# Seeding the second of seven block products in PSUM, and one order of products and down words for every block of a feed-forward network

## The chip, the cores and the metric

The kernel runs on one core of one Trainium2 chip. The metric is device time in microseconds, the median of several executions. The profile is of one execution. Its engines are named as the profile names them: PE (TensorE, matmuls), PEld (its weight loads), DVE (VectorE), ACT (ScalarE), POOL (GpSimd) and SP (the queue from which most DMA transfers are issued).

## The reference

Two layers, each of a feed-forward network, a mixer and a second feed-forward network, with a layer norm behind each. There are 256 tokens of width 1024, all in float32. The change is in the four feed-forward networks:

```python
def swiglu(x, w_in, w_out):          # w_in: 1024 x 5632, w_out: 2816 x 1024
    gu = x @ w_in
    g, u = gu[..., :D_FF], gu[..., D_FF:]
    return (jax.nn.silu(g) * u) @ w_out

x = layer_norm(ALPHA * x + 0.5 * swiglu(x, ffn_w_in[l, 0], ffn_w_out[l, 0]), ...)
```

The mixers (an mLSTM in layer 0, windowed attention in layer 1) are left alone.

## The kernel before

**Numbers.** Each float32 operand of a matmul is held as two parts, a rounded high part and a low part, which is the remainder. `mm3` (lines 617 to 620) makes a product of three matmuls: high by high, high by low, low by high. A weight word is a tile of 128 x 1024 elements (512 KB). It arrives by DMA into `w_raw` or `s_raw`, ACT casts it to `w_hi`, and DVE subtracts to get `w_lo`. One word feeds 12 matmuls of 512 columns, whether as a quarter of a wide product or as a row of the down projection (a "down word").

**A feed-forward network** (`ffn`, lines 770 to 1052). It begins with the first 512 columns of gate and up (8 words), goes on with 256 more of both (4 words, the "middle"), and does the other 2048 of each in four blocks of 512 (`seven`, lines 946 to 1006). The down projection has 22 words. They are put between the products one by one (`down`, lines 914 to 926), and six are left for the tail, where the layer norm is.

**A block** computes gate and up for both halves of the tokens by seven products in place of eight. Its words are b11 (gate, upper half), b12 (up, upper), b21 (gate, lower) and b22 (up, lower), two words each. The products use sums of words: b11 gets b12, then b22 added by DVE (`s_raw<-s_raw,s_raw`), and is split anew each time. After that DMA adds b21 to it (a transfer on POOL's queue that accumulates). The sums of x on the other side (`S1` to `S4`) are made once per network. The order before is: product 1 (into bank `qa`), `before()`, which turns the last rows of the block ahead by four PE transposes, product 2 (into `qc`), one down word, the products with `S1` (into `qb`) and `S2` (onto `qa`), one down word, those with `S3` and `S4`, one down word, the last product with b11 as DMA has left it, four transposes (`tr`), one down word. The last block of a network leaves out the last two down words. Two down words stand between the middle and block 0.

The gate of the first half of the tokens is product 1 plus product 2. Product 1 is also needed in `qa`, where the `S2` product is added onto it. Before the change ACT copies `qa` to SBUF (`e1`), DVE adds `qc` to it, and ACT takes the Silu of the sum:

```python
def end1():
    v["g0"] = copied(qa, "e1")
def end2():
    W.when_ready(lambda: nc.vector.tensor_add(v["g0"], v["g0"], qc), qc)
```

**What sets the order.** Each engine runs its own list in order. While a network is recorded, `Paced` (lines 65 to 167) keeps a reckoning of when each engine would be done, and after every matmul `Weights.fill` (lines 376 to 400) decides whether a cast, a subtraction or a sum of words is put into the lists of ACT and DVE, earliest due first. The due times follow from `plan`, the list of splits in the order of their use, which the outer `seven` (lines 492 to 524) writes. `Weights.load` (lines 223 to 251) issues the transfers, also by first use. In a network's first part it takes an `s_raw` word only if its place in the plan is less than 12 (`FIRST`) ahead of the words used.

Of the kernel before, what the change touches and what calls it, by code (L numbers as in the profile page):

```python
# [23 lines left out]
SEVENS = 4  # L24
# [40 lines left out]
class Paced:  # L65
# [94 lines left out]
            self.mark(o, self.act + 125)  # L160

    def on_tensor(self, name, n, out, ins):
        self.pe = max(self.pe, self.when(*ins)) + (109.0 if name == "transpose" else n / 2.4 + 13.3)
        for o in out:
            self.mark(o, self.pe + 200)
        if self.filler is not None:
            self.filler()
# [277 lines left out]
def trunk_kernel(ctx: ExitStack, tc: tile.TileContext, x, ffn_w_in, ffn_w_out, ln_g, ln_b, ml_w_in, ml_gate_b,  # L445
# [46 lines left out]
    def seven(w, c0, c1, n, down):  # L492

        def at(r0, c):
            return [two(w, r0 + 256 * j, c) for j in range(2)]

        b12, b11, b22 = ([word(x, 2, TAGS[r]) for x in at(*p)]
                         for r, p in ((2, (0, c1)), (4 if n % 2 else 1, (0, c0)), (3, (512, c1))))
        b21 = at(512, c0)
        full = n < SEVENS - 1  # L500
        half = 1360.0
        s1 = [split_of(w_, None, None, half) for w_ in b11]
        for j in range(2):
            after[s1[j]] = [(b11[j], b12[j]), (b12[j], at(512, c1)[j])]
        for a in b21:
            piece(a, 2, None, half)
        down(1)
        t1 = [split_of(w_, None, p, half, BY_SUM) for w_, p in zip(b11, s1)]
        for j in range(2):
            after[t1[j]] = [(b11[j], b22[j])]  # L510
        t2 = [split_of(w_, None, p, half, BY_SUM) for w_, p in zip(b11, t1)]
        for j in range(2):
            after[t2[j]] = [(b11[j], b21[j])]
        down(1)
        for w_, p in zip(b12, s1):
            split_of(w_, None, p, half, BY_MOVE)
        for w_ in b22:
            split_of(w_, None, None, half)
        if full:
            down(1)  # L520
        for w_, p in zip(b11, t2):
            split_of(w_, None, p, half, BY_MOVE)
        if full:
            down(1)

    ends = {}
    for j, (kind, l, i, _) in enumerate(stages):
        if kind == "ffn":
            wi, wo = ffn_w_in[l, i], ffn_w_out[l, i]
            nth = iter(range(2 * UNITS))  # L530

            def down(n):
                for _ in range(n):
                    rows(wo, next(nth))

            for c0 in (0, F):
                for a in range(4):
                    wide(wi, a * 256, c0)
            for a in range(4):
                beside(wi, a * 256, 512, F + 512)  # L540
            down(2)
            for g in range(SEVENS):
                c0 = 768 + 512 * g
                seven(wi, c0, F + c0, g, down)
            down(6)
        elif kind == "mlstm":
            for c0 in (1024, 1536):
                for a in range(4):
                    wide(ml_w_in[0], a * 256, c0)
            for c0 in range(0, 1024, 256):  # L550
                for a in range(2):
                    narrow(ml_w_in[0], a * 512, c0)
            for c0 in (2048, 2560):
                for a in range(4):
                    wide(ml_w_in[0], a * 256, c0)
            for c in range(8):
                rows(ml_w_out[0], c, (lambda c=c: gcol[:, c:c + 1]))
        else:
            for c0 in (1024, 0):
                for a in range(4):  # L560
                    wide(at_w_in[0], a * 256, c0)
            for c0 in (512, 768):
                for a in range(2):
                    narrow(at_w_in[0], a * 512, c0)
            for c in range(8):
                rows(at_w_out[0], c)
        ends[j] = len(words)
# [28 lines left out]
    nc.vector.tensor_scalar(ident, ji, 0.0, None, op0=OP.is_equal)  # L596
    mhalf = consts.tile([128, 2], F32, name="mhalf")
    nc.gpsimd.memset(mhalf, -0.5)

    gcol = consts.tile([128, 8], F32, name="gcol")  # L600
    gw = consts.tile([128, 8, 16], F32, name="gw")
# [168 lines left out]
    def ffn(l, i, n, pending, last):  # L770
        with ExitStack() as ph:
# [18 lines left out]
            def tr(hB, t, h):  # L790
                p = wbank((128, 4, 128))
                for k in range(4):
                    nc.tensor.transpose(p[:, k], h[:, k * 128:(k + 1) * 128], ident)
                split_evac(pair(hB, A, A, tok(t)), p, wait=True)

            def chunks(hB, n_):
# [117 lines left out]
            def down(n_):  # L914
                if not y:
                    y.extend([ybank() for _ in range(2)] for _ in range(2))
                W.flush()
                for _ in range(n_):
                    c = done_[0]
                    w, = W.take(1)  # L920
                    for t in range(2):
                        for o in range(2):
                            mm3(y[t][o], pair(hT[c], A, tok(t)), pair(w, A, 0, slice(o * 512, o * 512 + 512)),
                                c == 0, False)
                    W.done()
                    done_[0] += 1
# [3 lines left out]
            def product(bank, x_of, first, then):  # L930

                for j in range(2):
                    w, = W.take(1)
                    for k in range(2):
                        mm3(bank, x_of(2 * j + k), pair(w, A, k), first and j == k == 0, j == k == 1, not first)
                then()
                W.done()

            def copied(bank, name):
                e = temp(name)  # L940
                nc.scalar.copy(e, bank)
                return e
# [3 lines left out]
            def seven(full, before):  # L946

                of = lambda k0, t: (lambda k: pair(xT, A, k0 + k, tok(t)))
                sum_ = lambda name: (lambda k: pair(xs[name], A, k))
                v = {}  # L950
                hB = h_room(4)
                chunks(hB, 4)
                qa, qc = wbank(), wbank()

                def end1():
                    v["g0"] = copied(qa, "e1")

                def end2():
                    W.when_ready(lambda: nc.vector.tensor_add(v["g0"], v["g0"], qc), qc)

                def end5():
                    v["u1"] = copied(qb, "e5")

                def end6():
                    v["u0"] = copied(qa, "e2")
                    W.flush()
                    nc.scalar.activation(v["g0"], v["g0"], AF.Silu)

                def end7():
                    W.when_ready(lambda: nc.vector.tensor_sub(v["u1"], v["u1"], qa), qa)  # L970

                def end3():
                    W.flush()
                    W.when_ready(lambda: nc.vector.tensor_sub(v["u0"], qb, v["u0"]), qb)
                    W.when_ready(lambda: nc.vector.tensor_mul(v["u0"], v["g0"], v["u0"]))

                def end4():
                    v["g1"] = temp("g1")
                    nc.scalar.activation(v["g1"], qa, AF.Silu)
                    W.flush()  # L980
                    tr(hB, 0, v["u0"])
                    W.when_ready(lambda: nc.vector.tensor_mul(v["u1"], v["g1"], v["u1"]), v["g1"])

                product(qa, of(0, 0), True, end1)
                before()
                if not full:
                    gb.extend(load_ln(lambda name: W.room(name, TAGS[1]), l, n))
                product(qc, of(4, 0), True, end2)
                down(1)
                qb = wbank()  # L990
                product(qb, sum_("S1"), True, end5)
                product(qa, sum_("S2"), False, end6)
                down(1)
                product(qa, sum_("S3"), False, end7)
                product(qb, sum_("S4"), False, end3)
                if full:
                    down(1)
                product(qa, of(4, 1), False, end4)
                if full:
                    down(1)  # L1000

                def second():
                    W.flush()
                    tr(hB, 1, v["u1"])

                return second
# [21 lines left out]
                nc.vector.tensor_mul(hh[t], sg, ps[t][:, 256:512])  # L1028
            hp = h_room(2)
            chunks(hp, 2)  # L1030
            down(1)

            def turn():
                p = wbank((128, 2, S))
                for t in range(2):
                    for k in range(2):
                        nc.tensor.transpose(p[:, k, tok(t)], hh[t][:, k * 128:(k + 1) * 128], ident)
                split_evac(hp, p, wait=True)

            down(1)  # L1040
            for g in range(SEVENS):
                turn = seven(g < SEVENS - 1, turn)
            if start:
# [592 lines left out]
```

## Time and profile before

| | |
|---|---|
| time, median of 3 runs | 913.22 us (913.14 to 914.09) |
| span of the profiled execution | 911.7 us |
| time of the profiled execution | not listed apart from its span; the median is 1.5 us above the span |
| PE busy | 902.5 us (99%), 4459 matmuls |
| DVE busy | 804.4 us (88%), 971 instructions |
| ACT busy | 573.1 us (63%) |
| POOL busy | 152.5 us (17%) |
| moved by DMA | 208.53 MB, 229 GB/s on average |

A busy time counts an engine's executing instructions. The idle time of an engine that nothing waits for costs nothing. In rows of the timeline the first number is the start and the second how long the row (with its count) lasts, both in microseconds.

### The profile page before, as it was taken

The numbers are of one execution on the slowest core, as the hardware profiler recorded it, in microseconds if no ns is written. First come the engines' busy times: TensorE is split into PE (matmuls) and PEld (weight loads), VectorE is DVE, ScalarE is ACT, GpSimd is POOL, SyncE is SP. The second block draws the span as 40 slices with busy tenths as digits, with TensorE's granted clock in tenths as the row PEclk, the third lists the DMA queues.
The fourth block names the chain that finished last, engine by engine and source line by source line (L and its number), as shares of the span: only waits on it lengthen the run. The fifth ranks groups of instructions, "written<-read, shape, count | busy, mean of one in ns | idle before, by whom it ended". The sixth has DMA issues, their size and how long they took to land.

```text
span 911.7 us, 12563 instructions
## 1 busy us (share of the span) xinstructions
PE 902.5 (99%) x4459; PEld 757.4 (83%) x4459; DVE 804.4 (88%) x971; ACT 573.1 (63%) x793; POOL 152.5 (17%) x192
## 2 busy tenths in 40 slices
PE   9999999999999999999999999999999999999996
PEld 7888888889988888888888888888898888888885
DVE  5999999886799898999888899998869889899886
ACT  5776777356664656776646676764569566676660
POOL 0111123113211011212011111110425301111110
PEclk9999999999999999999999999999999999999999
DMA  8999998546637898997868989986534587899851
GB/s 281 367 328 259 288 274 215 162 137 186 208 111 246 296 234 244 290 285 234 241 193 269 259 257 283 272 223 197 159 119 140 163 293 221 204 298 278 252 138 47
DMA packets 100703, 208.53 MB, mean 229 GB/s; under 512 B 6904, under 2 KB 21264, under 8 KB 100640
## 3 DMA queue, kind: packets, MB, share of 16 engines
q1 hardware_dynamic: 82368, 173.04, 54.2%
q0 software_dynamic: 17696, 33.65, 22.3%
q10 hardware_dynamic: 576, 1.05, 0.3%
q8 instruction: 35, 0.57, 0.3%
q14 instruction: 28, 0.23, 0.1%
HBM read 206.65 MB, written 1.05 MB: 228 GB/s over the span
## 4 chain that ended last, share of the span: by engine, by line
PE 98%; DVE 1%; DMA 0%; issue 0%; DVEq 0%
PE pw L180 64%; PE py L180 35%; DMA x<-in_x_dram 0%; DVE x L180 0%; DVE stats L180 0%; DVEq L1632 0%; DVE mv L180 0%; DVE rs L180 0%
## 5 line engine op out<-in xcount | busy, mean ns | idle before, releaser
L180 DVE TENSOR_TENSOR w_lo<-w_raw,w_hi 128x1024 fp32r<-128x1024 f32 (+1 forms) x213 | 255.2, 1219 | 26.6 <-ACT w_hi L180 24.8
L180 ACT CAST w_hi<-w_raw 128x1024 fp32r<-128x1024 f32 (+1 forms) x213 | 218.9, 1049 | 80.3 <-PE py L180 21.7
L180 DVE TENSOR_TENSOR w_lo<-s_raw,w_hi 128x1024 fp32r<-128x1024 f32 x192 | 228.6, 1219 | 18.3 <-ACT w_hi L180 18.2
L180 ACT CAST w_hi<-s_raw 128x1024 fp32r<-128x1024 f32 x192 | 196.6, 1054 | 58.4 <-PE py L180 23.3
L180 PE MATMUL pw<-w_hi,xT_hi 128*128 128x512 f32 x480 | 189.5, 396 | 0.0
L180 PE MATMUL pw<-w_hi,xT_lo 128*128 128x512 f32 x480 | 187.0, 391 | 0.0
L180 PE MATMUL pw<-w_lo,xT_hi 128*128 128x512 f32 x480 | 186.7, 390 | 0.0
L122 POOL DMA_DIRECT2D s_raw<-in_ffn_w_in_dram x64 | 77.4, 1211 | 484.1 <-DVE s_raw L180 226.3
L180 PE MATMUL py<-w_hi,h_hi 128*128 128x512 f32 x349 | 138.2, 396 | 0.0
L180 PE MATMUL py<-w_hi,h_lo 128*128 128x512 f32 x349 | 136.2, 390 | 0.0
L180 PE MATMUL py<-w_lo,h_hi 128*128 128x512 f32 x349 | 136.0, 390 | 0.0
L180 PEld LDWEIGHTS pw<-w_hi,xT_lo 128*128 128x128 f32 x480 | 90.0, 188 | 19.1
L180 PEld LDWEIGHTS pw<-w_lo,xT_hi 128*128 128x128 f32 x480 | 90.3, 188 | 18.6 <-DVE w_lo L180 1.2
L180 PEld LDWEIGHTS pw<-w_hi,xT_hi 128*128 128x128 f32 x480 | 90.1, 188 | 17.4 <-ACT w_hi L180 0.2
L180 PE MATMUL pw<-w_hi,S_hi 128*128 128x512 f32 x256 | 99.7, 390 | 0.0
L180 PE MATMUL pw<-w_lo,S_hi 128*128 128x512 f32 x256 | 99.7, 389 | 0.0
L180 PE MATMUL pw<-w_hi,S_lo 128*128 128x512 f32 x256 | 99.7, 389 | 0.0
L180 PEld LDWEIGHTS py<-w_hi,h_lo 128*128 128x128 f32 x349 | 65.5, 188 | 14.1
L180 DVE TENSOR_TENSOR s_raw<-s_raw,s_raw 128x1024 f32<-128x1024 f32 x64 | 76.8, 1219 | 0.3
L180 PEld LDWEIGHTS py<-w_lo,h_hi 128*128 128x128 f32 x349 | 65.7, 188 | 13.0
L180 PEld LDWEIGHTS py<-w_hi,h_hi 128*128 128x128 f32 x349 | 65.6, 188 | 12.7
L180 PEld LDWEIGHTS pw<-w_hi,S_lo 128*128 128x128 f32 x256 | 48.1, 188 | 10.0
(205 smaller groups left out, 1122.7 us busy)
## 6 DMA issues: line engine op xcount, KB each, us to landing
s_raw<-in_ffn_w_in_dram SPq DMA_DIRECT2D x96, 512.0 KB, 8.0
w_raw<-in_ffn_w_out_dram SPq DMA_DIRECT2D x88, 512.0 KB, 6.1
w_raw<-in_ffn_w_in_dram SPq DMA_DIRECT2D x64, 512.0 KB, 5.7
s_raw<-in_ffn_w_in_dram POOLq DMA_DIRECT2D x64, 512.0 KB, 8.3
w_raw<-in_ml_w_in_dram SPq DMA_DIRECT2D x24, 512.0 KB, 4.6
w_raw<-in_ffn_w_in_dram SPq DMA_DIRECT2D x32, 256.0 KB, 6.0
w_raw<-in_at_w_in_dram SPq DMA_DIRECT2D x12, 512.0 KB, 4.8
w_raw<-in_ml_w_out_dram SPq DMA_DIRECT2D x8, 512.0 KB, 4.1
```

The source lines that it names most:

```text
L122: self.nc.gpsimd.dma_start(ap, source, accum_op=OP.add)
L180: r = f(out, *args, **kw)
```

## The change

1. ACT copies product 1 from `qa` to `qc`, PSUM to PSUM. Product 2 is accumulated onto that copy, its first matmul without the flag that starts an accumulation. ACT takes the Silu from `qc` as soon as the `S1` product is done. `e1` and DVE's add are gone.
2. The transposes of `tr` and `turn` are issued with the start flag on the first of a bank only (`turn_in`).
3. A block is now: product 1, down word, `before()`, product 2, `S1`, `S2`, down word, `S3`, `S4`, down word, last product, transposes, down word. All four blocks have four down words, and there are none between the middle and block 0. The plan of words is written in the same order.
4. The reckoning takes 109 ns for every PE instruction of 128 columns, in place of those named transpose.

```diff
     def on_tensor(self, name, n, out, ins):
-        self.pe = max(self.pe, self.when(*ins)) + (109.0 if name == "transpose" else n / 2.4 + 13.3)
+        self.pe = max(self.pe, self.when(*ins)) + (109.0 if n == 128 else n / 2.4 + 13.3)
...
+        down(1)
         for a in b21:
             piece(a, 2, None, half)
-        down(1)
...
-        if full:
-            down(1)
+        down(1)
         for w_, p in zip(b11, t2):
             split_of(w_, None, p, half, BY_MOVE)
-        if full:
-            down(1)
+        down(1)
...
                 beside(wi, a * 256, 512, F + 512)
-            down(2)
...
+    def turn_in(o, a, k):
+        nc.tensor.matmul(o, a, ident, is_transpose=True, start=k == 0, stop=True, skip_group_check=k > 0)
...
                 def end1():
-                    v["g0"] = copied(qa, "e1")
+                    nc.scalar.copy(qc, qa)
 
                 def end2():
-                    W.when_ready(lambda: nc.vector.tensor_add(v["g0"], v["g0"], qc), qc)
+                    pass
 
                 def end5():
+                    v["g0"] = temp("g0")
+                    nc.scalar.activation(v["g0"], qc, AF.Silu)
                     v["u1"] = copied(qb, "e5")
 
                 def end6():
                     v["u0"] = copied(qa, "e2")
                     W.flush()
-                    nc.scalar.activation(v["g0"], v["g0"], AF.Silu)
...
                 product(qa, of(0, 0), True, end1)
+                down(1)
                 before()
...
-                product(qc, of(4, 0), True, end2)
-                down(1)
+                product(qc, of(4, 0), False, end2)
                 qb = wbank()
                 product(qb, sum_("S1"), True, end5)
                 product(qa, sum_("S2"), False, end6)
                 down(1)
                 product(qa, sum_("S3"), False, end7)
                 product(qb, sum_("S4"), False, end3)
-                if full:
-                    down(1)
+                down(1)
                 product(qa, of(4, 1), False, end4)
-                if full:
-                    down(1)
+                down(1)
...
             hp = h_room(2)
             chunks(hp, 2)
-            down(1)
...
-            down(1)
             for g in range(SEVENS):
                 turn = seven(g < SEVENS - 1, turn)
```

**Where instructions move.** The first place is DVE in the first part of the kernel, around the two products `hh` that end the first 512 columns of network 0. `pw_276` to `pw_279` are the banks of those columns, `S4` the last sum of x, and `w_raw_235` is the tenth word of the network (the second of the middle). Before:

```order
L180 TENSOR_TENSOR w_lo_341<-s_raw0_211,w_hi_315 128x1024
L180 TENSOR_TENSOR S4_347<-py_171,S2_319 128x512
L180 TENSOR_TENSOR w_lo_357<-w_raw_235,w_hi_334 128x1024
L180 TENSOR_TENSOR S4_lo_350<-S4_347,S4_hi_349 128x512
L180 TENSOR_TENSOR hh_365<-sg_272,pw_276 128x512
L180 TENSOR_TENSOR hh_375<-sg_274,pw_277 128x512
L180 TENSOR_TENSOR s_raw0_211<-s_raw0_211,s_raw1_223 128x1024
L180 TENSOR_TENSOR w_lo_395<-w_raw_254,w_hi_343 128x1024
```

After, where the tenth word is `w_raw_239` and the next one `w_raw_260`:

```order
L180 TENSOR_TENSOR S4_353<-py_173,S2_321 128x512
L180 TENSOR_TENSOR w_lo_364<-s_raw0_215,w_hi_338 128x1024
L180 TENSOR_TENSOR S4_lo_356<-S4_353,S4_hi_355 128x512
L180 TENSOR_TENSOR hh_367<-sg_274,pw_278 128x512
L180 TENSOR_TENSOR hh_377<-sg_276,pw_279 128x512
L180 TENSOR_TENSOR w_lo_388<-w_raw_239,w_hi_349 128x1024
L180 TENSOR_TENSOR s_raw0_215<-s_raw0_215,s_raw1_227 128x1024
L180 TENSOR_TENSOR w_lo_406<-w_raw_260,w_hi_372 128x1024
```

The low part of the tenth word has moved from ahead of the two `hh` to behind them, and both words of block 0's b11 (`s_raw0`) are split ahead of it in place of one.

The second place is ACT from the end of product 1 of block 0 in network 0 to the Silu of its gate. `pw_546` and `pw_500` are `qa` before and after, `pw_501` is `qc`, and `h_hi_491` and `h_hi_496` are the casts of the rows that `before()` turns. Before:

```order
L180 COPY e1_567<-pw_546 128x512
L180 CAST h_hi_491<-pw_569 128x512
L180 CAST w_hi_581<-s_raw0_257 128x1024
L180 CAST w_hi_593<-s_raw1_270 128x1024
L180 CAST w_hi_607<-s_raw2_361 128x1024
L180 CAST w_hi_618<-s_raw2_387 128x1024
L180 CAST w_hi_630<-w_raw_435 128x1024
L180 COPY e5_650<-pw_623 128x512
L180 CAST w_hi_654<-w_raw_465 128x1024
L180 CAST w_hi_660<-s_raw3_509 128x1024
L180 COPY e2_672<-pw_546 128x512
L180 ACTIVATE e1_567<-e1_567 128x512
```

After:

```order
L180 COPY pw_501<-pw_500 128x512
L180 CAST w_hi_526<-w_raw_408 128x1024
L180 CAST w_hi_536<-s_raw0_215 128x1024
L180 CAST w_hi_547<-s_raw1_205 128x1024
L180 CAST h_hi_496<-pw_549 128x512
L180 CAST w_hi_561<-s_raw1_227 128x1024
L180 CAST w_hi_575<-s_raw2_305 128x1024
L180 CAST w_hi_587<-s_raw2_333 128x1024
L180 CAST w_hi_598<-w_raw_419 128x1024
L180 ACTIVATE g0_604<-pw_501 128x512
L180 COPY e5_606<-pw_579 128x512
```

The copy's target is the bank that product 2 is added to, and the Silu now stands ahead of the copy of the `S1` product.

The third place is SP's list of transfers in the first microseconds, from the seventh word of network 0 on. Before:

```order
L118 DMA w_raw_201<-in_ffn_w_in_dram 128x2x512
L118 DMA w_raw_209<-in_ffn_w_in_dram 128x2x512
L118 DMA s_raw0_211<-in_ffn_w_in_dram 128x2x512
L116 DMA w_raw_220<-in_ffn_w_in_dram 128x2x256 x2
L118 DMA s_raw1_223<-in_ffn_w_in_dram 128x2x512
L116 DMA w_raw_235<-in_ffn_w_in_dram 128x2x256 x2
L116 DMA w_raw_254<-in_ffn_w_in_dram 128x2x256 x2
```

After:

```order
L118 DMA s_raw0_161<-in_ffn_w_in_dram 128x2x512
L118 DMA w_raw_203<-in_ffn_w_in_dram 128x2x512
L118 DMA s_raw1_205<-in_ffn_w_in_dram 128x2x512
L118 DMA w_raw_213<-in_ffn_w_in_dram 128x2x512
L118 DMA s_raw0_215<-in_ffn_w_in_dram 128x2x512
L116 DMA w_raw_224<-in_ffn_w_in_dram 128x2x256 x2
L118 DMA s_raw1_227<-in_ffn_w_in_dram 128x2x512
L116 DMA w_raw_239<-in_ffn_w_in_dram 128x2x256 x2
```

Block 0's words now come ahead of the words of the middle: four of them stand ahead of the tenth word in place of two.

More of the change, by code (lines that the diff above doesn't have):

```diff
@@ L499, in seven @@
         b21 = at(512, c0)
-        full = n < SEVENS - 1
         half = 1360.0
@@ L792, in tr @@
                 for k in range(4):
-                    nc.tensor.transpose(p[:, k], h[:, k * 128:(k + 1) * 128], ident)
+                    turn_in(p[:, k], h[:, k * 128:(k + 1) * 128], k)
                 split_evac(pair(hB, A, A, tok(t)), p, wait=True)
@@ L1036, in turn @@
                     for k in range(2):
-                        nc.tensor.transpose(p[:, k, tok(t)], hh[t][:, k * 128:(k + 1) * 128], ident)
+                        turn_in(p[:, k, tok(t)], hh[t][:, k * 128:(k + 1) * 128], 2 * t + k)
                 split_evac(hp, p, wait=True)
-            down(1)
             for g in range(SEVENS):
```

## The prediction

> **What bounds the kernel now.** I read the page first, for the busy times.
>
> ```profile
> span 911.7 us, 12563 instructions
> PE 902.5 (99%) x4459; PEld 757.4 (83%) x4459; DVE 804.4 (88%) x971; ACT 573.1 (63%) x793; POOL 152.5 (17%) x192
> ```
>
> PE is busy for all but 9.2 us. A modelled busy time can hide stalls, so the chain of waits comes next: the shares by line, and its pieces from the end of network 0's middle on (start, length, what).
>
> ```profile
> by line: PE pw L180 63.7%; PE py L180 34.7%; DMA x<-in_x_dram 0.5%; DVE x L180 0.3%; DVE stats L180 0.2%; issue 0.1%; DVEq L1632 0.1%; DVE mv L180 0.0%; DVE rs L180 0.0%
> ...
> 42.61 5.44 PE py L180 x24
> 48.05 5.93 PE pw L180 x28
> 53.98 2.72 PE py L180 x12
> 56.70 5.44 PE pw L180 x24
> ```
>
> 98.4% of the span is PE following PE. 24 matmuls in 5.44 us are 227 ns each, so a word (12 matmuls) is 2.72 us, and products and down words alike run at that rate with nothing between them. The third view is PE's and PEld's waits by what they wait for (total, times, longest).
>
> ```profile
> PE py L180 <- DVE ident L180: 1.7, 1, 1.7
> ...
> PEld pw L180 <- DVE w_lo L180: 1.5, 4, 0.4
> ```
>
> The first is the start. The second says that in the whole run only four low parts came late. So the time is the number of matmuls times their rate, plus a start and an end that the change does not touch.
>
> What could become the bound is DVE. One block of network 0 in the view by stretches, and two stretches in which that network's words arrive (PE, PEld, DVE, ACT, POOL, clock, DMA share, GB/s):
>
> ```profile
> 15.00:20.00 5.00, 5.00 (x23) 4.13 (x22) 3.55 (x4) 2.58 (x4) 0.00 (x0) 1.00 0.86 243
> 20.00:25.00 5.00, 5.00 (x24) 4.13 (x23) 3.68 (x6) 3.91 (x6) 0.00 (x0) 1.00 1.04 365
> 109.64:140.52 30.88, 30.88 (x141) 25.57 (x140) 30.67 (x31) 21.65 (x25) 4.81 (x4) 1.00 0.97 281
> ```
>
> In that block DVE is busy for 30.67 of 30.88 us. It keeps up by being ahead. From 20 us on DMA is full as well: at 365 GB/s a word of 524,288 bytes takes 1.44 us.
>
> **The change part by part.** PE first. The list of PE has the same 4459 matmuls and transposes before and after, in another order, so the sum for PE is zero at an unchanged rate.
>
> *What goes.* The groups that the seeding touches (count, busy, mean ns):
>
> ```profile
> L180 ACT COPY e<-pw 128x512 f32<-128x512 f32 x48 | 28.2, 587 | 40.3 <-PE pw L180 39.9
> ...
> L180 DVE TENSOR_TENSOR e<-e,pw 128x512 f32<-128x512 f32 x32 | 21.8, 680 | 0.0
> ...
> L180 ACT ACTIVATE e<-e 128x512 f32<-128x512 f32 x16 | 10.1, 634 | 0.0
> ...
> L180 ACT ACTIVATE g<-pw 128x512 f32<-128x512 f32 x16 | 9.6, 600 | 28.7 <-PE pw L180 28.7
> ```
>
> Of the 32 adds into `e`, 16 are the gate's: 16 x 0.680 = 10.9 us of DVE go, 0.68 a block. ACT keeps 48 copies, 16 of them now to PSUM, and 16 Silus read PSUM at 600 ns in place of SBUF at 634: half a microsecond less. None of that is on PE's path, so by itself it brings nothing. It gives DVE slack, and that is worth what late low parts cost now. One of the four is plain, at the last product of a block in network 2 (PE, and DVE's low part of that word):
>
> ```profile
> 563.49 0.39 PE L180 MATMUL pw<-w_hi,xT_hi 128*128 128x512 f32 x1
> 563.90 0.50 PE L180 MATMUL pw<-w_lo,xT_hi 128*128 128x512 f32 x1
> 564.24 0.40 PE L180 MATMUL pw<-w_hi,xT_lo 128*128 128x512 f32 x1
> ...
> 562.62 1.22 DVE L180 TENSOR_TENSOR w_lo<-s_raw,w_hi 128x1024 fp32r<-128x1024 f32 x1
> ```
>
> The low part ends at 563.84; the steps of PE are 0.41 and 0.34 in place of 0.227, so 0.3 us are lost. With 0.68 us a block less ahead of it that goes: -0.3.
>
> *The new wait.* Product 2 now waits for ACT's copy. Between product 1 and it stands a down word, 2.72 us, as cover. Copies of `qa` start when PE ends unless a cast ahead of them waits. The worst of the sixteen (two rows of ACT, two of PE):
>
> ```profile
> 540.24 1.05 ACT L180 CAST w_hi<-s_raw 128x1024 fp32r<-128x1024 f32 x1 [3.10 <-DVE s_raw L180]
> 541.20 0.57 ACT L180 COPY e<-pw 128x512 f32<-128x512 f32 x1
> ...
> 539.68 0.39 PE L180 MATMUL pw<-w_hi,xT_lo 128*128 128x512 f32 x1
> 539.91 0.60 PE L180 MATMUL pw<-ident,e 128*128 128x128 f32 x4
> ```
>
> Product 1 ends at 540.07, the copy at 541.77: 1.70 us, a microsecond under the cover. A copy to PSUM is in no trace; it is bounded by zero and by the longest row of that size here, the sum of 0.680, and I take 0.587, its nearest row. All lie under the cover, so this is +0. The Trainium skill (PSUM — Partial Sum Buffer, section Engine vs sequencer instructions) says that ScalarE's queue is strictly first in, first out; the copy that began 1.13 us late behind a waiting cast agrees.
>
> *The order.* From block to block the sequence only turns: the down word behind product 2 now stands ahead of it, and `S1` comes at the same place. That is +0, and the last block's two more down words are cover for it. What changes is block 0: the two down words ahead of it are gone, so its products come up to 5.44 us earlier against the middle (the row at 42.61). In networks 1 to 3 the words are split far ahead; in network 0 everything arrives at DMA's rate. There three things are tight.
>
> First, the tenth word. DVE around the two `hh`, and PE at that word:
>
> ```profile
> 29.48 1.22 DVE L180 TENSOR_TENSOR w_lo<-w_raw,w_hi 128x1024 fp32r<-128x1024 f32 x1
> ...
> 31.22 1.28 DVE L180 TENSOR_TENSOR hh<-sg,pw 128x512 f32<-128x512 f32 x2
> 32.41 1.22 DVE L180 TENSOR_TENSOR s_raw<-s_raw,s_raw 128x1024 f32<-128x1024 f32 x1
> 33.55 1.22 DVE L180 TENSOR_TENSOR w_lo<-w_raw,w_hi 128x1024 fp32r<-128x1024 f32 x1
> ...
> 33.38 0.39 PE L180 MATMUL pw<-w_hi,xT_hi 128*128 128x512 f32 x1
> 33.61 0.39 PE L180 MATMUL pw<-w_lo,xT_hi 128*128 128x512 f32 x1
> ```
>
> Its low part was made at 29.48 to 30.70, 2.9 us ahead of PE at 33.61. Behind the `hh` it takes the place of the sum at 32.41 and ends at 33.63, just late. One long operation more stands ahead of the `hh` (a sum and two splits of block 0's words come in, against one split before, and the tenth word goes out), 1.14 us from start to start (32.41 to 33.55). DVE's idle moments there may or may not take it up. So the wait is 0 to 1.2 us; I take 0.5. Four words of block 0 in place of two ahead in SP's list are up to 2 x 1.44 = 2.9 us more for DMA; the first can use the room that DMA has before 20 us (243 GB/s), so I count one, and the cast still ends ahead of 32.4.
>
> Second, the turn of the last 256 columns, `hh` of the middle:
>
> ```profile
> 44.29 0.75 DVE L180 TENSOR_TENSOR hh<-sg,pw 128x256 f32<-128x256 f32 x2 [0.38 <-ACT sg L180]
> ...
> 50.61 0.60 PE L180 MATMUL pw<-ident,hh 128*128 128x128 f32 x4
> 50.97 0.48 PE L180 MATMUL pw<-w_hi,xT_hi 128*128 128x512 f32 x1
> 51.28 0.39 PE L180 MATMUL pw<-w_lo,xT_hi 128*128 128x512 f32 x1
> ```
>
> It moves ahead by one word, from 50.61 to 47.9, and `hh` is there at 45.04: +0, with two operations (2.3 us) to spare.
>
> Third, block 0's last product, which needs b11 after three rounds of DVE and a transfer. DVE and PE at its second word:
>
> ```profile
> 72.17 1.22 DVE L180 TENSOR_TENSOR w_lo<-s_raw,w_hi 128x1024 fp32r<-128x1024 f32 x1
> ...
> 74.45 0.39 PE L180 MATMUL pw<-w_lo,xT_hi 128*128 128x512 f32 x1
> ```
>
> PE now wants it at 74.45 - 5.44 = 69.0. In the new list 28 long operations, itself among them, and 8 short ones stand behind the first `hh`: 28 x 1.14 + 6 x 0.6 + 2 x 0.37 = 36.3 us, where I take 0.6 for a 512-column operation from start to start (the two `hh` at 31.22 end after 1.28) and 0.37 for a 256-column one. From 32.41 that ends at 68.7, from 1.1 us later at 69.8, and any idle adds. So 0 to 1.5 us; I take 0.5.
>
> Start flags and the reckoning's 109 ns change no count of instructions: +0. Network 0 gives +1.0, the late word -0.3: span 911.7 + 0.7 = 912.4. The median of the runs lies 1.5 us above the span (913.22), so I predict 913.9.
>
> **The rivals.**
>
> *Network 0 stalls for more* (slower). Same mechanism, at the upper ends: 1.2 + 1.5, and another microsecond if the turn's cover goes too because DMA is late by both words. That is 911.7 - 0.3 + 3.7, so 916.6 in the runs' terms. For it: DMA and DVE both full there. Against it: a wait of PE lets DVE and DMA catch up for whatever comes next.
>
> *The copy gates product 2* (slower). Place: 16 products. Point: a copy that ends over 2.72 us (3.1 with the transposes) behind product 1. A copy of 1.7 us or more, or casts that wait over 2 us, would do it; if all blocks were late by 0.3 us that is 4.8, so 918. Against it: the worst of sixteen was 1.70, and DVE, on which that one waited, gets lighter. If one wait reached several microseconds, the Trainium skill (TensorE: Matmul & The Clock Gate, Part 1) has a clock gate that halves PE's clock after an idle window of about 3.4 us; no row of these blocks shows such an idle time, and the clock column reads 1.00 in both stretches above.
>
> *The transposes get cheaper* (faster). After each group of transposes PE's second step is longer: 50.97 to 51.28, 0.31 in place of 0.227. If that came from start flags and went with them, 44 groups (11 a network, two in the first columns, one for the middle, eight in the blocks) x 0.087 = 3.8 us, so 909.4 + 0.7 = 910.1. Against it: the step is behind the group, not within it, and the four transposes keep their kind.
>
> *It does nothing:* DVE's relief is real but hidden, network 0 holds: 911.7 - 0.3, so 912.9.
>
> **How the numbers follow.** A measurement of this kernel can tell about 0.2% from no change, 1.8 us. My forecast of 913.9, with "it does nothing" as its lower end, has a chance of 0.74 and its own range is 912.6 to 915.0. Network 0 stalling for more has 0.13, the copy as a gate 0.07, cheaper transposes 0.06. So slower 0.20, within 0.2% 0.74, faster 0.06. The range for 8 in 10 is 912.6 to 916.2: the forecast, and half of the first rival.
>
> **What would show it.** Right: DVE loses 16 adds (about 793 us busy); PE's waits on low parts all lie ahead of 75 us, at the tenth word and at block 0's last product, together about 1 us; no PE step above 0.35 us at product 2; 227 ns a matmul everywhere; the wait at 563 gone. Wrong: a row in which a `pw` matmul waits for ACT's copy in many blocks, a wait of PE over 2 us in network 0, or another step length behind transposes.

## The result and the profile after

The changed kernel took 915.76 us (median of 20 runs, 914.38 to 918.3) against 913.45 for the kernel before in the same session (912.85 to 914.9): a ratio of 1.0024, 95% interval 1.0017 to 1.0031. The profiled execution had a span of 915.0 us, 3.3 more than before, and ran 1.0 us above the median. So the change costs some 0.24%.

The page's first lines:

```profile
span 915.0 us, 12548 instructions
PE 903.0 (99%) x4459; PEld 757.2 (83%) x4459; DVE 796.4 (87%) x955; ACT 577.1 (63%) x793; POOL 152.8 (17%) x192
```

PE has the same 4459 instructions and the same busy time within 0.5 us. DVE has 16 operations and 8.0 us less. So what the change set out to save was saved, and the time rose all the same. The view of waits says where (total, times, longest):

```profile
PEld pw L180 <- DVE w_lo L180: 5.4, 6, 1.7
PE pw L180 <- DVE w_lo L180: 3.3, 3, 1.4
```

Before, low parts made only PEld wait, 1.5 us in all. Now three of them stop PE. All three are in network 0, in PE's timeline (start, length, what, idle time before it):

```profile
27.28 0.47 PE L180 MATMUL pw<-w_hi,xT_hi 128*128 128x512 f32 x1
29.10 0.50 PE L180 MATMUL pw<-w_lo,xT_hi 128*128 128x512 f32 x1 [1.35 <-DVE w_lo L180]
...
34.45 0.39 PE L180 MATMUL pw<-w_hi,xT_hi 128*128 128x512 f32 x1
35.50 0.50 PE L180 MATMUL pw<-w_lo,xT_hi 128*128 128x512 f32 x1 [0.67 <-DVE w_lo L180]
...
70.81 0.39 PE L180 MATMUL pw<-w_hi,xT_hi 128*128 128x512 f32 x1
72.49 0.50 PE L180 MATMUL pw<-w_lo,xT_hi 128*128 128x512 f32 x1 [1.29 <-DVE w_lo L180]
```

From start to start a matmul takes 0.227 us; here it takes 1.82, 1.05 and 1.68, and the step behind each is 0.11 longer as well. So they cost 1.70, 0.94 and 1.56 us: 4.2. The late word at 563 us is gone (-0.3), and this run's first matmul came 0.6 us earlier than in the run of before (6.3 us; over all runs it starts between 6.3 and 7.3, so that is chance). 4.2 - 0.3 - 0.6 = 3.3, the whole difference of the spans.

What made each word late is on ACT and DVE (ACT's cast of the eighth word is the row at 26.14):

```profile
17.39 1.05 ACT L180 CAST w_hi<-w_raw 128x1024 fp32r<-128x1024 f32 x1 [3.04 <-DMA w_raw<-in_ffn_w_in_dram]
20.04 1.05 ACT L180 CAST w_hi<-w_raw 128x1024 fp32r<-128x1024 f32 x1 [1.59 <-DMA w_raw<-in_ffn_w_in_dram]
21.00 1.04 ACT L180 CAST w_hi<-s_raw 128x1024 fp32r<-128x1024 f32 x1
...
25.61 0.63 ACT L180 CAST S_hi<-S 128x512 fp32r<-128x512 f32 x1 [0.73 <-DVE S L180]
26.14 2.00 ACT L180 CAST w_hi<-w_raw 128x1024 fp32r<-128x1024 f32 x2
...
27.83 1.22 DVE L180 TENSOR_TENSOR w_lo<-w_raw,w_hi 128x1024 fp32r<-128x1024 f32 x1
...
34.23 1.22 DVE L180 TENSOR_TENSOR w_lo<-w_raw,w_hi 128x1024 fp32r<-128x1024 f32 x1
...
63.25 1.23 DVE L180 TENSOR_TENSOR s_raw<-s_raw,s_raw 128x1024 f32<-128x1024 f32 x1 [1.50 <-DMA s_raw<-in_ffn_w_in_dram]
64.74 1.22 DVE L180 TENSOR_TENSOR s_raw<-s_raw,s_raw 128x1024 f32<-128x1024 f32 x1 [0.27 <-DMA s_raw<-in_ffn_w_in_dram]
...
71.22 1.22 DVE L180 TENSOR_TENSOR w_lo<-s_raw,w_hi 128x1024 fp32r<-128x1024 f32 x1
```

The same cast in the run of before:

```profile
22.59 1.05 ACT L180 CAST w_hi<-w_raw 128x1024 fp32r<-128x1024 f32 x1
```

ACT waits for the transfers of the sixth and the seventh word (3.04 and 1.59 us), then casts one of block 0's words, which is new there (21.00). A cast of a sum of x (25.61), which waits for DVE, has moved ahead of the eighth word's as well, so that ACT comes to the eighth word 3.5 us later than before. Its low part ends at 29.05, and PE wanted it at 27.5. The tenth word's low part (34.23) stands behind `hh`, as foreseen. The third wait is at block 0's last product. There DVE stood idle for 1.77 us at sums of block 1 whose words had not landed, and the wanted low part is queued behind them.

The seed cost nothing. Its groups by form (count, busy, mean ns, idle before):

```profile
L180 DVE TENSOR_TENSOR e<-e,pw 128x512 f32<-128x512 f32 x16 | 10.9, 680 | 0.0
L180 ACT COPY pw<-pw 128x512 f32<-128x512 f32 x16 | 9.2, 575 | 15.2 <-PE pw L180 15.1
```

The latest of the 16 copies ended 1.29 us behind product 1, 1.4 us under the cover of a down word, and no row of PE waits for one.

### The profile page after: what moved, and what is told of

Its sections match the earlier page's. It is cut to its first block, busy times and chain, and to the rows that moved or that the text cites. A ratio compares the mean times of both kernels' runs of the same rounds, so it can differ in the third digit from the quotient of the medians.

```text
span 915.0 us, 12548 instructions
## 1 busy us (share of the span) xinstructions
PE 903.0 (99%) x4459; PEld 757.2 (83%) x4459; DVE 796.4 (87%) x955; ACT 577.1 (63%) x793; POOL 152.8 (17%) x192
## 3 DMA queue, kind: packets, MB, share of 16 engines
q10 hardware_dynamic: 576, 1.05, 0.3%
HBM read 206.65 MB, written 1.05 MB: 227 GB/s over the span
## 4 chain that ended last, share of the span: by engine, by line
PE 92%; DVE 4%; DMA 2%; issue 1%; ACT 0%; DVEq 0%; POOL 0%; POOLq 0%
PE pw L180 58%; PE py L180 34%; DVE w_lo L180 2%; DMA w_raw<-in_ffn_w_in_dram 1%; DMA s_raw<-in_ffn_w_in_dram 1%; DVE s_raw L180 0%; DVE x L180 0%; DVE h_lo L180 0%; DVE stats L180 0%; DVE hh L180 0%; DVE e L180 0%; ACT xT_hi L180 0%; ACT w_hi L180 0%; DVE S_lo L180 0%; DVEq L1628 0%
## 5 line engine op out<-in xcount | busy, mean ns | idle before, releaser
L180 ACT CAST w_hi<-w_raw 128x1024 fp32r<-128x1024 f32 (+1 forms) x213 | 219.6, 1050 | 72.2 <-PE py L180 27.5
L180 PEld LDWEIGHTS pw<-w_hi,S_hi 128*128 128x128 f32 x256 | 48.1, 188 | 10.0
```

The lines of the kernel that those rows point to most:

```text
L180: r = f(out, *args, **kw)
```

## The experiments

Three theories stood. A and B: new order and all, what is lost is lost in network 0, by words that come late there. For A all three waits come from block 0's words being fetched earlier; for B the third comes from the down words that no longer stand ahead of block 0. C: the seed (copy, wait, flags) costs something in every block. All runs below are against the kernel before in the same session (913.3 to 913.4 us).

**The order alone.** The changed kernel without the seed: `e1` copied to SBUF, DVE's add, the Silu from SBUF and the start flags (of product 2 and of all transposes) put back.

```diff
-                    nc.scalar.copy(qc, qa)
+                    v["g0"] = copied(qa, "e1")
...
-                    pass
+                    W.when_ready(lambda: nc.vector.tensor_add(v["g0"], v["g0"], qc), qc)
...
-                product(qc, of(4, 0), False, end2)
+                product(qc, of(4, 0), True, end2)
```

> The change without the seeding: the copy into e1, DVE's 16 adds and the Silu from SBUF are as before, all transposes have the start flag, and the order of products and down words is the changed one. Theories A and B: the three waits of network 0 are there (3.5 to 5.5 us in sum), DVE has 16 adds more, and the time is 915.8 to 917. Rival C: 913.4, as before the change.

Measured: 915.34 us, ratio 1.0025 (1.0015 to 1.0034), a little under the range expected. The loss is there without the seed, so C falls.

The profiled execution is the slowest of the nine, 2.3 us above their median. Up to 47 us its lists of SP, ACT and DVE are those of the changed kernel, and yet there is no wait at the eighth word and one of only 0.12 us at the tenth. What differs is when words landed. ACT's casts of the seventh and, with the one behind it, of the eighth word:

```profile
18.22 1.05 ACT L180 CAST w_hi<-w_raw 128x1024 fp32r<-128x1024 f32 x1 [2.15 <-DMA w_raw<-in_ffn_w_in_dram]
...
24.32 2.00 ACT L180 CAST w_hi<-w_raw 128x1024 fp32r<-128x1024 f32 x2
```

The changed kernel had the seventh word at 20.04 us, and two more runs below with these lists (no cover; the change in network 0 alone) at 20.12 and 20.40, each with a wait at the eighth word of 1.1 us or more. So the first two waits need late words besides the new lists. Why the same list of transfers lands later in one execution than in another is open, and how often it does was not measured.

What is lost in this execution is nearly all at block 0's last product (PE, then one stretch with PE's granted clock third from the end):

```profile
69.02 0.39 PE L180 MATMUL pw<-w_hi,xT_hi 128*128 128x512 f32 x1
71.92 0.50 PE L180 MATMUL pw<-w_lo,xT_hi 128*128 128x512 f32 x1 [2.51 <-DVE w_lo L180]
...
73.18 0.88 PE L180 MATMUL pw<-ident,e 128*128 128x128 f32 x4
...
74.28 0.63 PE L180 MATMUL py<-w_lo,h_hi 128*128 128x512 f32 x1
74.71 0.63 PE L180 MATMUL py<-w_hi,h_lo 128*128 128x512 f32 x1
...
72.00:75.00 3.00, 3.00 (x12) 2.54 (x13) 2.42 (x3) 1.50 (x3) 0.00 (x0) 0.73 1.09 246
```

The wait is 2.67 us beyond a matmul's step, longer than with the seed. That does not show that taking DVE's adds away helps there: the low part ends at 71.86 us, 0.6 earlier than with the seed, but PE, which had not been stopped before, wants it 1.8 earlier. And behind it something came that nobody had priced: from 73.2 us on the steps are 0.43 in place of 0.227, until 76.8. That is PE's clock (0.73 here, 0.71 in the next 3 us), and against the same instructions of the changed kernel it costs 1.6 us more.

**Where: network 0 alone, and all but network 0.** One kernel keeps the old order in network 0, with its two down words ahead and its sums on DVE, and has the change in networks 1 to 3. The other is the complement. Both switch the lines of the order and of the seed, and keep the transposes' flags and the 109 ns:

```diff
+            old = start          # the complement: not start
...
-                down(1)
+                if not old:
+                    down(1)
                 before()
...
-                product(qc, of(4, 0), False, end2)
+                product(qc, of(4, 0), old, end2)
+                if old:
+                    down(1)
```

> The changed kernel, but network 0 keeps the old order, its two down words ahead of block 0 and its sums on VectorE; networks 1 to 3 have the new order and the seed. Theory (all of the loss is network 0's): the three waits there go, the late word at 563 us stays away: 913.3 - 0.3 = 913.0, between 912.7 and 913.4. Rival (order or seed costs something in every block): three quarters of the 2.4 us stay, 915.1.

> The complement: network 0 in the new order with the seed, networks 1 to 3 as before. Theory (all of the loss is network 0's): 913.3 + 2.4 to 4.2 = 915.7 to 917.5, with waits for low parts of 2.7 to 4.2 us ahead of 75 us. Rival (order or seed costs something in every block): a quarter of 2.4 us, 913.9.

Measured: 912.97 us with the change in networks 1 to 3, ratio 0.9996 (0.9987 to 1.0005); 916.41 us with the change in network 0, ratio 1.0026 (1.0016 to 1.0035). All of the loss is network 0's. The rest of the change is free, and worth nothing that can be measured. PE's waits for low parts in the first kernel, and then in the second:

```profile
PE pw L180 <- DVE w_lo L180: 0.6, 1, 0.6
```

```profile
PE pw L180 <- DVE w_lo L180: 2.7, 3, 1.1
```

The second has the three waits of the changed kernel, at 28, 35 and 71 us. In the first those three are gone, as expected, but it has one of 0.83, at 74 us, where DVE's list is that of before but ran 1.5 us later. The old order stands at the edge there too.

**The window for loads.** `FIRST` is how far ahead, counted in words of the plan, block words may be loaded at the start. With 10, SP's first transfers are again those of before.

```diff
-FIRST = 12
+FIRST = 10
```

> The changed kernel with FIRST 10 in place of 12: block 0's s_raw words of each network are fetched as late, counted in words used, as they were before the change. The before runs at 913.45, the change at 915.76, with three waits of PE in network 0 (eighth word 1.7 us, tenth 0.9, block 0's last product 1.6). Theory A, all three waits come from the earlier fetch: no PE wait over 0.3 us in network 0, and 913.1. Theory B, the first two come from the earlier fetch and the third from the 5.44 us of down words that no longer stand ahead of block 0: the first two go, the third stays at 1.5 to 2.5 us, and 914.4 to 915.4. Rival C, the seeding itself costs the time: 915.8 as in the change.

Measured: 914.60 us, ratio 1.0010 (1.0002 to 1.0019). The first two waits are gone and the third stays, now in two pieces (0.90 and 0.78 us, and 0.11 behind each: 1.9):

```profile
67.22 0.39 PE L180 MATMUL pw<-w_hi,xT_hi 128*128 128x512 f32 x1
68.35 0.50 PE L180 MATMUL pw<-w_lo,xT_hi 128*128 128x512 f32 x1 [0.74 <-DVE w_lo L180]
...
69.61 0.39 PE L180 MATMUL pw<-w_hi,xT_hi 128*128 128x512 f32 x1
70.62 0.50 PE L180 MATMUL pw<-w_lo,xT_hi 128*128 128x512 f32 x1 [0.62 <-DVE w_lo L180]
```

That is theory B: the waits at the eighth and tenth words go with block 0's words being fetched and split earlier, and the one at 70 us does not. One execution without the first two is not enough to say so, since the order alone had one too; the time speaks for it, with a ratio of 1.0010 where the change had 1.0024.

**DVE's list at 70 us.** In that run DVE has no idle time at all from 30 to 72 us. The next kernel takes two of its sums out ahead of the late low parts, and keeps the planner's reckoning, so that every other instruction stands where it stood.

```diff
-        nc.vector.tensor_add(t, t, self.raw[v])
+        self.nth_sum = getattr(self, "nth_sum", -1) + 1
+        if self.nth_sum in (4, 5):
+            nc.on_vector("tensor_add", D, [t], [t, self.raw[v]])
+        else:
+            nc.vector.tensor_add(t, t, self.raw[v])
```

> The changed kernel with the narrower window for loads at the start (10 in place of 12), and two of VectorE's sums left out in network 0, block 1's first, which stood at 61.74 and 63.48 us ahead of the low parts that came late at 67 and 69 us. The lists of all engines are otherwise the same. Theory (there VectorE has no idle time and its list is too long): 2 x 1.14 = 2.3 us less ahead of these low parts, over the 1.9 us of the waits: they go, 914.6 - 1.9 = 912.7. Rival (the transfers or the casts set these low parts): VectorE waits in place of adding, the waits stay at 1.5 to 1.9 us, 914.6.

Measured: 913.70 us, ratio 1.0002 (0.9994 to 1.0011): 0.9 us of the 1.9 went. The first piece is gone, the second stays at 0.86. DVE's timeline says why:

```profile
61.85 0.69 DVE L180 TENSOR_TENSOR e<-e,pw 128x512 f32<-128x512 f32 x1 [1.15 <-PE pw L180]
62.46 1.22 DVE L180 TENSOR_TENSOR w_lo<-w_raw,w_hi 128x1024 fp32r<-128x1024 f32 x1
64.58 0.69 DVE L180 TENSOR_TENSOR e<-pw,e 128x512 f32<-128x512 f32 x1 [0.90 <-PE pw L180]
...
65.91 1.22 DVE L180 TENSOR_TENSOR w_lo<-s_raw,w_hi 128x1024 fp32r<-128x1024 f32 x1
...
68.18 1.22 DVE L180 TENSOR_TENSOR w_lo<-s_raw,w_hi 128x1024 fp32r<-128x1024 f32 x1
```

The 2.3 us that were freed became 2.05 us of idle time: DVE now waits for products of PE at the two evictions, and the low parts stand behind them. So both expectations were half right. Its list was too long by about 1 us; that the rest is its order is read from these rows and was not run apart.

**One down word back ahead of block 0.** In the plan and in the code one of the two returns, and the last block gives up its last one.

```diff
+            down(1)
             for g in range(SEVENS):
...
-        down(1)
+        if full:
+            down(1)
```

> The changed kernel with one down word put back ahead of block 0 (in the plan and in the code), the last block of each network without its last down word. Half of what block 0 lost in lead, and its fetch one word later. Theory A and theory B: the waits in network 0 come down from 4.2 us in sum to 1 to 3 us, 913.8 to 915.2. Rival C: all seeds are in it, 915.8.

Measured: 915.54 us, ratio 1.0021 (1.0013 to 1.0030). That is over the range expected. The third wait is gone, as B has it. The eighth word's is gone too; its cast stands ahead of block 0's again. The tenth word's is 1.40 us. PE's start, 0.4 us later, and a stop of 0.3 at 346 us make up most of the rest of the profiled execution's loss. Two words ahead weren't tried.

**Both remedies.** `FIRST = 10` and one down word ahead.

> The changed kernel with two remedies for network 0 together: the narrower window for loads at the start (10 in place of 12; alone it took the waits at the eighth and the tenth word away) and one down word put back ahead of block 0 (alone it took the wait at block 0's last product away). Theory (each wait has its own cause, and the remedies add): no wait over 0.3 us ahead of 80 us, 0.3 us at most elsewhere, 912.9 to 913.3. Rival (VectorE's list is too long in network 0 whatever is moved, so that a wait taken away comes back later): 1 us or more of waits there, 914.3 or more.

Measured: 919.88 us, ratio 1.0067 (1.0053 to 1.0081). The theory that the remedies add failed badly. In the profiled execution, 1.3 us above the median, the first two waits are gone, but a longer one has come (DVE, then PE, then two stretches with DMA's share and GB/s last):

```profile
64.82 1.23 DVE L180 TENSOR_TENSOR s_raw<-s_raw,s_raw 128x1024 f32<-128x1024 f32 x1 [1.80 <-DMA s_raw<-in_ffn_w_in_dram]
...
71.61 0.40 PE L180 MATMUL pw<-w_hi,xT_hi 128*128 128x512 f32 x1
76.22 0.79 PE L180 MATMUL pw<-w_lo,xT_hi 128*128 128x512 f32 x1 [4.21 <-DVE w_lo L180]
...
20.00:25.00 5.00, 5.00 (x23) 4.13 (x22) 3.63 (x5) 3.59 (x8) 0.00 (x0) 1.00 0.83 248
...
75.00:80.00 5.00, 3.78 (x11) 3.10 (x12) 3.44 (x4) 0.99 (x2) 0.00 (x0) 0.54 1.06 348
```

Between 20 and 25 us DMA now moves 248 GB/s, where the changed kernel moved 378: 0.65 MB, over one word, that has to come later. DVE then stands for 1.80 us at a sum whose word has not landed, the last product waits 4.4 us, and PE's clock is down behind it (0.54), which costs another 2.8. Block words fetched too early can stop the eighth word; fetched too late, block 0's last product. That a down word ahead takes one of the ten places of the window, so that block words are asked for later, is argued and was not run apart.

**No cover.** The down word goes back behind product 2, so that nothing stands between product 1 and the product that waits for its copy.

```diff
                 product(qa, of(0, 0), True, end1)
-                down(1)
                 before()
...
                 product(qc, of(4, 0), False, end2)
+                down(1)
```

> The changed kernel with the down word back behind product 2, in the plan and the code: between product 1 and the product 2 that is added to ACT's copy stand only the four transposes. It prices the copy as a gate. Theories A and B: a copy ends 0.61 us behind product 1, the four transposes take 0.36, so PE waits 0.25 to 0.5 us at each of 16 products, 4 to 8 us in sum, on top of what network 0 loses: 919 to 924. If the copy is no gate at all: 915.8.

Measured: 925.46 us, ratio 1.0128 (1.0112 to 1.0143), a little over the range. The waits:

```profile
PEld pw L180 <- ACT pw L180: 6.0, 13, 0.5
PE pw L180 <- DVE hh L180: 3.0, 3, 1.0
PE pw L180 <- ACT pw L180: 2.9, 13, 0.2
```

In 13 blocks product 2 comes 0.49 us late (6.4 us). In the three others, block 0 of networks 1 to 3, the turn of the middle stands there and waits for `hh`, some 1.15 us each (3.5). The rest is network 0's. That is the price of the copy as a gate, and what the moved down word buys.

**Flags and reckoning alone.** The kernel before with only the transposes' start flags (`turn_in`) and the planner's 109 ns.

> The kernel before with only the transposes' start flags and the planner's 109 ns of the change. Theory (network 0's words come late, flags and reckoning are free): as before, 913.3 us, the second matmul step behind a group of transposes still 0.31 us. Rival (transposes get cheaper with the flags): 44 groups x 0.087 = 3.8 us less, 909.5, with that step at 0.23. Rival (the reckoning moves instructions so that words come late): over 914.

Measured: 913.45 us, ratio 0.9998 (0.9990 to 1.0007). No instruction changed its place. The second matmul behind a group of transposes is still 0.31 us behind the first:

```profile
50.83 0.48 PE L180 MATMUL pw<-w_hi,xT_hi 128*128 128x512 f32 x1
51.14 0.40 PE L180 MATMUL pw<-w_lo,xT_hi 128*128 128x512 f32 x1
```

**What a wait costs by its length.** The kernel before, with chains of small ACT copies behind product 1 in networks 1 to 3, whose last result PE transposes.

```diff
+                    nc.scalar.copy(slow[0], bank[:, 0:128])
+                    for j in range(n_):
+                        nc.scalar.copy(slow[(j + 1) % 2], slow[j % 2])
+                    nc.tensor.transpose(wbank((128, 4, 128))[:, 0], slow[n_ % 2], ident)
```

> The kernel before with waits of known length put on PE: in networks 1 to 3, behind product 1 of blocks 0 and 2, a chain of 3, 6, 9, 12, 15 and 18 small copies on ScalarE whose last result PE transposes. With some 0.24 us a copy PE waits about 1.0, 1.7, 2.4, 3.1, 3.9 and 4.6 us. It asks from which wait on PE's clock falls. Theory (the idle window of 3.4 us of the Trainium skill): 227 ns a matmul behind the first four waits, half rate behind the last two only: 913.3 + 16.7 + 2 x 1.6 = 933. Rival (as in the run of the order alone, where it fell behind a wait of 2.7 us): 227 ns behind the first two or three, half rate behind the others: 935 to 937.

Measured: 945.54 us. A copy took 0.30 us, not 0.24, so the waits were longer than meant: 1.72, 2.65, 3.69, 4.63, 5.67 and 6.60 us beyond a step. The second and the third, each with the first matmuls behind it:

```profile
396.43 0.39 PE L181 MATMUL pw<-w_hi,xT_lo 128*128 128x512 f32 x1
399.31 0.33 PE L181 MATMUL pw<-ident,slow 128*128 128x128 f32 x1 [2.49 <-ACT slow L181]
...
400.14 0.39 PE L181 MATMUL pw<-w_lo,xT_hi 128*128 128x512 f32 x1
400.38 0.39 PE L181 MATMUL pw<-w_hi,xT_lo 128*128 128x512 f32 x1
...
513.18 0.39 PE L181 MATMUL pw<-w_hi,xT_lo 128*128 128x512 f32 x1
517.10 0.38 PE L181 MATMUL pw<-ident,slow 128*128 128x128 f32 x1 [3.53 <-ACT slow L181]
...
518.56 0.63 PE L181 MATMUL pw<-w_lo,xT_hi 128*128 128x512 f32 x1
518.99 0.63 PE L181 MATMUL pw<-w_hi,xT_lo 128*128 128x512 f32 x1
```

Behind 1.72 and 2.65 us PE goes on at full rate (400.14 to 400.38). Behind 3.69 and more the next steps are 0.43, and the slow stretch costs 1.6, 1.6, 1.6 and 2.3 us. 25.0 us of waits and 7.1 behind them are 32.1 of the 32.2 us measured.

## Why the prediction was right, and where it was not

The number held: 915.76 lies in the range, 1.9 us above the forecast. But it is outside the likeliest case's own range (912.6 to 915.0). What happened is the first rival, network 0 stalling for more, at nearly its size (916.6). The range held because half of that rival had been put into it, and not because the sum was right: it had 1.0 us of waits, and 4.2 came in the profiled execution.

- **PE unchanged:** right; 4459 instructions, and no slower step outside network 0.
- **DVE's relief is worth only the late word at 563:** right that it is worth no more; with the change in networks 1 to 3 alone the time is that of before. That the late word went because of it is not shown. It is gone as well in the run of the order alone, which keeps the adds, and in that of flags and reckoning, whose lists are those of before and where another low part, at 626 us, costs 0.6. DVE's busy time fell by 8.0 us and not by 10.9: the lengths of its operations add up to 10.4 less, but a busy time counts a stretch in which two overlap once, and they overlap by 2.4 less (58.4 us after, 60.8 before).
- **ACT half a microsecond lighter:** right by the lengths of its operations, which add up to 625.2 us after and 626.1 before. Its busy time rose by 4.0 us all the same, because they overlap by some 5 us less; that cost nothing.
- **The copy costs +0 under a down word:** right. It took 0.575 us where 0.587 was taken. Without the cover it would have been the second rival: 925.46.
- **Turn of `hh`, start flags, 109 ns:** right, +0 each; the transposes did not get cheaper.
- **The tenth word, 0.5:** right place, 0.94 measured, inside its bounds of 0 to 1.2; with the same lists but earlier words 0.12 (the order alone).
- **Block 0's last product, 0.5:** right place and too small: 1.56, just over the upper bound of 1.5. That it came so near is luck. The sum of the list, 36.3 us, fits, but the list began at 34.23 in place of 32.41 to 33.5, and of the "any idle adds", for which nothing was put in, 1.77 us came, at sums whose words had not landed. So the low part ended at 72.4, where 68.7 to 69.8 had been reckoned. PE, stopped twice before, wanted it at 71.0 and not at 69.0, and that hid 2.0 us.
- **A third place was missed,** the eighth word, 1.70 us in the profiled execution. This is the step that failed. "The first can use the room that DMA has before 20 us" was true (330 GB/s there, where it was 243), but only the tenth word was then looked at. SP's list, quoted in the section on the change, has one of block 0's words ahead of the seventh word and a second ahead of the eighth, and ACT had waited for the seventh already. ACT's list has one of their casts and one of a sum of x ahead of the eighth word's, and these moved instructions weren't counted. Alone they bring that cast 1.7 us later than before (24.32 and 22.59) and cost nothing, as the order alone shows; with the seventh word late as well it was 3.5. The argument against the rival, that one wait lets DVE and DMA catch up for the next, did not save the third.

## What to carry to other kernels

Work that is taken off an engine which is full but ahead is worth only the waits that it causes; here that was 0.3 us at most for 10.9. When an order is changed, the start is where it can be paid for, because nothing is ahead yet there: follow each moved transfer past every transfer that it overtakes, and not only to the one that was tight before. A list with two tight suppliers (here DMA and DVE) has no slack to move about: each remedy helped where it was aimed, and the two together were worse than either. And before a wait in one profiled execution is laid to the order of instructions, compare another execution with the same lists: two of the three waits here came and went with when words landed.

## What the runs showed of the hardware that was not expected

PE's clock fell behind a wait of 2.67 us (the order alone, granted clock 0.73 and 0.71) and not behind one of 2.65 us (the chains of copies, 1.00 in the 5 us behind it). Each was seen once. In the first case PE had gone on for 1.3 us at full rate before it fell; behind waits of 3.69 us and more it was down at once (0.66 in the 5 us behind the first of them). Each fall cost 1.6 to 2.8 us beside the wait. The Trainium skill (TensorE: Matmul & The Clock Gate, Part 1, What's actually happening) has a free-running window of about 3.4 us, of which one idle window halves the clock. The falls behind 3.69 us and more agree, if such a window lay whole within each wait. The fall behind 2.67 us does not agree with a window that has to be idle throughout; that it depends on where in the window the wait falls would fit both cases, and no run here shows the window itself. So a wait of PE between some 2.6 and 3.7 us should be priced with and without another 1.6 us.
